# Four single waits in a hybrid decoder step: other score banks, turns ahead of the last scores, forget sums turned at once, idle products at the start

## The chip, the cores and the metric

The kernel runs on one core of one Trainium2 chip. TensorE (PE in the profile, with its weight loads as PEld) multiplies matrices, VectorE (DVE), ScalarE (ACT) and GpSimd (POOL) do the element-wise work, and SyncE (SP) issues most transfers. PSUM, into which PE writes, has eight banks of 128 partitions x 512 float32. The metric is the device time of one execution in microseconds (us), as the median of several runs.

## The reference

One inference step of a two-layer decoder, for a prompt of 2048 positions and for 8 sequences of 4 new positions that have a paged past of 2048. Layer 0 runs two groups of four heads beside each other, a gated linear recurrence ("A") and a forgetting attention ("B", called fox in the code), both from one input projection. Layer 1 is a gated linear attention. Of what the change touches, the reference is this, shortened:

```python
def rmsnorm(x, g):
    y = xf * lax.rsqrt(jnp.mean(xf * xf, axis=-1, keepdims=True) + EPS)
    return y * g

def fox_prompt(q, k, v, log_f):                 # per head, blocks of 128 queries
    c = jnp.cumsum(log_f, axis=1)
    logits = q @ k.T * scale + c[:, None] - c[None, :]
    p = softmax(where(causal, logits, -inf))
    return p @ v

def fox_sample(...):                            # the new positions, on the pages
    suffix_past = lax.cumsum(lf_past, axis=1, reverse=True) - lf_past
    logit_past = q @ k_past.T * scale + cum_new[..., None] + suffix_past[:, :, None, :]
```

Every output is compared with this, in float32. The kernel multiplies float32 values as two float16 parts, a high and a low one, and so three products stand for one (lines L623, L624 and L625 of the kernel before; the helper is `mm3`).

## The kernel before, in words

The program has three stages: `phase_even` (norm of the input, the projections of layer 0 and the recurrence of A), `phase_fox` (the attention B), and the output projection with layer 1. Instructions are written down in one order by Python generators that are merged by estimated costs (the numbers that they yield), and a scheduler then sets each engine's order. Every engine works through its own row in order, and instructions wait for each other by semaphores. A tile with a tag takes the next of the buffers that the tag has; the pool gives a tag its PSUM banks at the first tile with that tag, from the first bank on that is free in the pool's region. A tile that reuses a bank waits for the last reader of the tile before it.

The start. Rows of x are loaded (`nx`), ACT squares them (`nsq`, L451), DVE multiplies them by the reciprocal root (L453), PE turns them in pieces of 128x128 (`nt`, L477), and ACT and DVE split them into the two float16 parts of `act` (L618, L619) with the gain `g_even`. The gain is first scaled by a power of two, for which PE spreads a row over the partitions (`spr_e`, L271) and DVE reduces it (L272). Meanwhile the first weight `w_Ai` is measured (`rm_Ai`, L300) and split (L353 on ACT, L354 on DVE). The first projection is `pt_Av`.

PSUM. In `phase_even` the pool has the tags "pj" (3 banks, the projections), "gr" (2), "st" (1) and "o" (2); the first tile is `spr_e` with "pj". The last projection is the value unit of B: four tiles `pt_Bv` turn over the three "pj" banks, and ACT (L1070) and DVE (L1064, L1071) read them out into `Bv` and `Bvs`. In `phase_fox` a pool that begins at the same first bank has "s" (2 banks, the scores) and "sc" (1, page scores), and another has "t" (2), "o" (1) and "kt" (2). The first tile of the former is a score tile with "s".

Attention. Sixteen groups (head h, group G of four blocks of 128 queries) are worked through. For a block, `scores` multiplies q and k (`s`), DVE adds the bias and takes the maximum (L1413), ACT takes exponentials (L1421, `L3150` is the piece 0 of block 15 of head 3), DVE sums and POOL normalizes (L1429). For a finished group, `values` turns the weights (`pt`, L1449), splits them (`th` on ACT, L1456; `tl` on DVE, L1457) and multiplies them with v into one bank `fo`, from which `fy` (DVE, L1472) reads it out. `values` turns two tiles ahead of the products. The values of a group run beside the scores of the next one; those of the last group run after its scores, in two halves of two blocks (`th3300` is the turn 0 of the first half of head 3 group 3; `th32011` is the turn 11 of head 3 group 2, the last one of that group). At this place ACT and DVE also prepare the output weights `w_o` (L353, L354, L360) and the activations `act` of the output projection (L1814, L1815).

Beside all that, `fox_sample` loads pages of the past with SP, turns the keys (`pkt`, L1573), copies them (`kts`, ACT and DVE) and scores them (`sc`). Between the pages it makes the sums of the log forget values: for each of the four heads it turns one 128x128 tile (`lfT`, L1620), copies it on ACT (`lfTs`, L1622) and multiplies it with two masks into `psf` (L1623, L1624).

## Time and profile before

| what | before |
|---|---|
| runs, median of 3 | 2329.38 us (2325.68 to 2329.55) |
| profiled execution, its own time | 2327.94 us |
| span of the profile | 2326.2 us |
| PE busy | 2248.9 us, 97% of the span |
| DVE, ACT, POOL busy | 1412.1, 1018.5, 733.7 us |
| mean granted clock | 0.991 |

A row of the profile names the start in us, the duration, the engine, the line of the kernel, the operation, the output and input tiles without their numbers, and their shapes. In square brackets stands the idle time of the engine before the row, and what ended it. A row with x4 is four instructions taken together. A stretch of the view by windows gives for each engine the busy time in it, then the mean TensorE clock that was granted (1.00 is full), the busy share of the transfer engines and their rate.

### The profile page before, as it was taken

The numbers are of one execution on the slowest core, as the hardware profiler recorded it, in microseconds if no ns is written. First come the engines' busy times: TensorE is split into PE (matmuls) and PEld (weight loads), VectorE is DVE, ScalarE is ACT, GpSimd is POOL, SyncE is SP. The second block draws the span as 40 slices with busy tenths as digits, with TensorE's granted clock in tenths as the row PEclk, the third lists the DMA queues.
The fourth block names the chain that finished last, engine by engine and source line by source line (L and its number), as shares of the span: only waits on it lengthen the run. The fifth ranks groups of instructions, "written<-read, shape, count | busy, mean of one in ns | idle before, by whom it ended". The sixth has DMA issues, their size and how long they took to land.

```text
span 2326.2 us, 57896 instructions
## 1 busy us (share of the span) xinstructions
PE 2248.9 (97%) x23060; PEld 1604.3 (69%) x23060; DVE 1412.1 (61%) x3281; ACT 1018.5 (44%) x2264; POOL 733.7 (32%) x786
## 2 busy tenths in 40 slices
PE   7999999999999999999999999999999999999998
PEld 5667677855755875565446888677677666666887
DVE  7766568526654657667777445366675655557554
ACT  6434354211222225555566543545544544545343
POOL 2333334001201214223345345144552432322232
PEclk9999999999999999999999999999999999999999
DMA  7343444755432377875983969524234431115553
GB/s 238 120 128 105 146 127 164 201 142 160 143 120 73 125 189 251 245 242 196 276 262 102 335 195 263 132 79 137 74 102 96 121 96 58 49 56 164 176 181 150
DMA packets 357423, 361.64 MB, mean 155 GB/s; under 512 B 105777, under 2 KB 300658, under 8 KB 353058
## 3 DMA queue, kind: packets, MB, share of 16 engines
q1 hardware_dynamic: 355010, 351.33, 49.4%
q0 software_dynamic: 2144, 6.62, 0.8%
q8 instruction: 181, 2.97, 0.5%
q14 instruction: 88, 0.72, 0.1%
HBM read 244.54 MB, written 96.42 MB: 147 GB/s over the span
## 4 chain that ended last, share of the span: by engine, by line
PE 40%; DVE 5%; DMA 2%; ACT 2%; issue 1%; POOL 1%; SPq 1%; POOLq 0%; DVEq 0%; ACTq 0%
PE pt_o L623 4%; PE pt_o L624 4%; PE pt_o L625 4%; PE pt_Cv L623 2%; PE pt_Cv L624 2%; PE pt_Cv L625 2%; PE o_C L910 1%; PE gl_C L756 1%; PE pt L1449 1%; PE pv L1711 1%; DMA yr<-yT 1%; DMA wr_Cv<-in_w_in_odd 1%; PE py_C L728 1%; DVE scT L771 1%; PE fo L623 0%
## 5 line engine op out<-in xcount | busy, mean ns | idle before, releaser
L623 PE MATMUL pt_o<-w_o,act 128*128 128x256 f16 x1024 | 278.9, 273 | 1.9 <-ACT sg1C L680 1.9
L624 PE MATMUL pt_o<-w_o,act 128*128 128x256 f16 x1024 | 278.9, 273 | 0.0
L625 PE MATMUL pt_o<-w_o,act 128*128 128x256 f16 x1024 | 278.7, 273 | 0.0
L623 PEld LDWEIGHTS <-act 128*128 128x128 f16 x2304 | 226.1, 98 | 35.9 <-issue 3.6
L624 PEld LDWEIGHTS <-act 128*128 128x128 f16 x2304 | 226.2, 98 | 32.0 <-issue 3.4
L625 PEld LDWEIGHTS <-act 128*128 128x128 f16 x2304 | 226.2, 98 | 29.9 <-issue 1.7
L790 POOL TENSOR_TENSOR kA<-kA,fA 128x512 f32<-128x512 f32 (+1 forms) x56 | 80.9, 1445 | 344.8 <-PE gl_A L756 273.1
L623 PE MATMUL pt_Cv<-w_Cv,act 128*128 128x256 f16 (+1 forms) x512 | 141.3, 276 | 0.0
L624 PE MATMUL pt_Cv<-w_Cv,act 128*128 128x256 f16 (+1 forms) x512 | 141.3, 276 | 0.0
L625 PE MATMUL pt_Cv<-w_Cv,act 128*128 128x256 f16 (+1 forms) x512 | 141.2, 276 | 0.0
L790 POOL TENSOR_TENSOR kC<-kC,fC 128x512 f32<-128x512 f32 (+1 forms) x56 | 83.6, 1492 | 154.3 <-PE gl_C L756 103.1
L1429 POOL TENSOR_SCALAR L<-L,nm 128x512 f32<-128x512 f32 (+3 forms) x160 | 99.3, 635 | 103.5 <-DVE nm L1425 46.7
L1421 ACT ACTIVATE L<-L,nm,kc 128x512 f32<-128x512 f32 (+3 forms) x160 | 118.2, 740 | 27.5 <-DVE nm L1419 26.3
L1456 ACT ACTIVATE th<-pt 128x512 f16<-128x512 f32 (+3 forms) x159 | 81.8, 528 | 88.3 <-PE pt L1449 86.8
L1457 DVE TENSOR_TENSOR tl<-pt,th 128x512 f16<-128x512 f32 (+3 forms) x159 | 95.0, 609 | 20.7 <-ACT th L1456 18.9
L1449 PE MATMUL pt<-ident,L 128*128 128x128 f32 x544 | 91.4, 280 | 1.4 <-POOL L L1429 0.9
L1573 PEld LDWEIGHTS pkt<-ident,pgcache_fox_k 128*128 128x128 f32 x512 | 59.2, 142 | 44.2 <-issue 27.1
L1573 PE MATMUL pkt<-ident,pgcache_fox_k 128*128 128x128 f32 x512 | 78.5, 281 | 5.7 <-DVE kts L1578 1.7
L1449 PEld LDWEIGHTS pt<-ident,L 128*128 128x128 f32 x544 | 67.7, 144 | 23.3 <-DVE tl L1457 4.5
L1911 ACT ACTIVATE vC<-pt_Cv,kc 128x512 f32<-128x512 f32 (+1 forms) x40 | 23.9, 598 | 129.9 <-PE pt_Cv L625 129.9
L623 PE MATMUL pt_Bk<-w_Bk,act 128*128 128x256 f16 x256 | 70.2, 274 | 1.8 <-DVE Bvs L1071 1.8
L623 PE MATMUL pt_Av<-w_Ai,act 128*128 128x256 f16 x256 | 70.8, 277 | 0.5 <-ACT act L618 0.5
(959 smaller groups left out, 6566.6 us busy)
## 6 DMA issues: line engine op xcount, KB each, us to landing
pgcache_fox_k<-in_cache_fox_k SPq DMA_DIRECT2D x128, 256.0 KB, 4.2
pgcache_fox_v<-in_cache_fox_v SPq DMA_DIRECT2D x128, 256.0 KB, 4.2
yr<-yT SPq DMA_DIRECT2D x16, 1024.0 KB, 7.4
x1d<-xo SPq DMA_DIRECT2D x44, 256.0 KB, 4.7
wr_o<-in_w_out_even SPq DMA_DIRECT2D x32, 256.0 KB, 5.3
xo<-in_x_prompt SPq DMA_DIRECT2D x32, 256.0 KB, 5.5
wr_Cv<-in_w_in_odd SPq DMA_DIRECT2D x32, 256.0 KB, 3.9
x1r<-x1d SPq DMA_DIRECT2D x16, 512.0 KB, 4.9
```

What stands on the lines that cost most here:

```text
L623: nc.tensor.matmul(ps, lh[0], rh[0], start=first, stop=False)
L624: nc.tensor.matmul(ps, lh[0], rh[1], start=False, stop=False)
L625: return nc.tensor.matmul(ps, lh[1], rh[0], start=False, stop=last)
L728: nc.tensor.transpose(py[:, c * rows : (c + 1) * rows], on[:rows, c, t * P : (t + 1) * P], self.ident[:rows, :rows])
L790: nc.gpsimd.tensor_tensor(kv[:, :, 0], kv[:, :, 0], t1.to_broadcast([P, nb, w]), ALU.mult)
L1421: self.last_exp = nc.scalar.activation(lt[:, :w], lt[:, :w], AF.Exp, bias=nm[:, 0:1], scale=ib, accum_out=nm[:, 2 + j : 3 + j])
L1429: nc.gpsimd.tensor_scalar(lt[:, :w], lt[:, :w], nm[:, 1:2], 2.0**14, ALU.mult, ALU.mult)
L1449: nc.tensor.transpose(pt[:, w : w + P], rows[b][s // 4][0][:, (s % 4) * P : (s % 4 + 1) * P], self.ident)
L1456: nc.scalar.activation(th[:, a:w], pt[:, a:w], AF.Copy),
L1457: nc.vector.tensor_tensor(tl[:, a:w], pt[:, a:w], th[:, a:w], ALU.subtract)))
L1573: last = nc.tensor.transpose(pk[:, j * P : (j + 1) * P], pgs[j][:, h * P : (h + 1) * P], self.ident)
L1911: r = nc.scalar.activation(v[h][:, g : g + cnt], ps[:, :, :256], AF.Copy, scale=c)
```

## The change

Four edits, in five places. As the kernel begins, a tile of zeros is set by DVE, and PE multiplies it by itself fifteen times into a PSUM tile with the tag "st" that nobody reads; and the second of the first row tiles is multiplied on ACT and not on DVE. Ahead of the attention, a tile `sc_first` with the tag "sc" is taken and not used, so that "sc" gets its bank before "s" does. In the last group, `values` of the first half is called after the third block's scores as far as its first two turns (`early`), and the rest of it follows after the last block's scores and the values of the group before; the bank `fo` is passed in a list, since it is taken later than the turns. And the four turns of the log forget values go into one tile, which DVE copies in one instruction, then the generator yields 3000, and then the eight products follow.

```diff
@@ norm_groups: prep
-                    nc.vector.tensor_scalar(xt[:n], xt[:n], r, None, ALU.mult)
+                    if c0 == P:
+                        nc.scalar.activation(xt[:n], xt[:n], AF.Copy, scale=r)
+                    else:
+                        nc.vector.tensor_scalar(xt[:n], xt[:n], r, None, ALU.mult)
@@ phase_even
+            warm = wp.tile([P, 512], F32, tag="kt", name="warm").bitcast(F16)
+            nc.vector.memset(warm[:, :512], 0.0)
+            ps = pps.tile([P, 512], F32, tag="st", name="warm")
+            for _ in range(15):
+                nc.tensor.matmul(ps, warm[:, :P], warm[:, :512], start=True, stop=True)
             self.sx_even = self.gain_scale(self.g_even, pps, "pj", "e")
@@ fox_prompt: values
-        def values(h, G, rows, po, b1, b2):
+        def values(h, G, rows, out, b1, b2, early=False):
...
             ahead = [turn(j) for j in range(min(2, nj))]
+            if early:
+                yield 0
+            po = out[0]
             for j in range(nj):
@@ fox_prompt: the groups
         groups = [(h, G) for h in range(NH) for G in range(4)]
+        pps.tile([P, 512], F32, tag="sc", name="sc_first")
         loads(0, 0)
...
+                if j + 1 == len(groups) and b == 2:
+                    po = []
+                    lead = values(h, G, rows, po, 0, 2, True)
+                    next(lead)
             yield from pv
-            po = pps.tile([P, 512], F32, tag="o", name=f"fo{h}{G}")
             if j + 1 < len(groups):
+                po = []
                 pv, ns = values(h, G, rows, po, 0, 4), 4 * (G + 1)
-
-        yield from values(h, G, rows, po, 0, 2)
+            po.append(pps.tile([P, 512], F32, tag="o", name=f"fo{h}{G}"))
+
+        yield from lead
         yield from values(h, G, rows, po, 2, 4)
@@ fox_sample: past
+            pt = pps.tile([P, 512], F32, tag="kt", name="lfT")
+            for h in range(NH):
+                nc.tensor.transpose(pt[:, h * P : (h + 1) * P], lfp[:, :, h], self.ident)
+            lt = fs.tile([P, 512], F32, tag="kt", name="lfTs")
+            nc.vector.tensor_copy(lt, pt)
+            yield 3000
             psf = pps.tile([P, NH, P], F32, tag="kt", name="psf")
             for h in range(NH):
-                pt = pps.tile([P, 512], F32, tag="kt", name=f"lfT{h}")
-                nc.tensor.transpose(pt[:, :P], lfp[:, :, h], self.ident)
-                lt = fs.tile([P, 512], F32, tag="kt", name=f"lfTs{h}")
-                nc.scalar.activation(lt[:, :P], pt[:, :P], AF.Copy)
-                nc.tensor.matmul(psf[:, h], lt[:, :P], stri, start=True, stop=False)
+                nc.tensor.matmul(psf[:, h], lt[:, h * P : (h + 1) * P], stri, start=True, stop=False)
```

The scheduler moves other instructions of the attention stage in consequence. The orders below are those that the two programs have; a row gives its place on the engine, the line, the operation and the tiles with the program's numbers. Lines of the changed kernel are a little further down (L1429 is the exponential that was L1421, L1464 the split that was L1456, L626 the product that was L623).

ACT at the end of head 3 group 2 and the start of the last group, before (`L315` are the exponentials of the last block, `th32` turns of group 2, `th33` turns of the last group):

```order
809 L1456 ACTIVATE th32010_18542<-pt32010_18539 128x256
810 L1456 ACTIVATE th32011_18647<-pt32011_18645 128x128
811 L1421 ACTIVATE L3150_18556,nm315_18633<-L3150_18556,nm315_18633,kc_67 128x512
812 L1421 ACTIVATE L3151_18598,nm315_18633<-L3151_18598,nm315_18633,kc_67 128x512
813 L1421 ACTIVATE L3152_18624,nm315_18633<-L3152_18624,nm315_18633,kc_67 128x512
814 L1421 ACTIVATE L3153_18630,nm315_18633<-L3153_18630,nm315_18633,kc_67 128x512
815 L1456 ACTIVATE th3300_18669<-pt3300_18664 128x512
816 L1456 ACTIVATE th3301_18678<-pt3301_18673 128x512
817 L353 ACTIVATE w_o000_18607<-wr_o000_18600,kc_67 128x512
```

And in the changed kernel:

```order
806 L1464 ACTIVATE th32010_18552<-pt32010_18549 128x256
807 L1464 ACTIVATE th3300_18564<-pt3300_18559 128x512
808 L1429 ACTIVATE L3150_18584,nm315_18641<-L3150_18584,nm315_18641,kc_67 128x512
809 L1429 ACTIVATE L3151_18590,nm315_18641<-L3151_18590,nm315_18641,kc_67 128x512
810 L1429 ACTIVATE L3152_18596,nm315_18641<-L3152_18596,nm315_18641,kc_67 128x512
811 L1429 ACTIVATE L3153_18602,nm315_18641<-L3153_18602,nm315_18641,kc_67 128x512
812 L353 ACTIVATE w_o000_18669<-wr_o000_18662,kc_67 128x512
813 L1464 ACTIVATE th3301_18573<-pt3301_18568 128x512
814 L353 ACTIVATE w_o000_18669<-wr_o000_18662,kc_67 128x512
815 L1464 ACTIVATE th32011_18655<-pt32011_18653 128x128
816 L360 ACTIVATE w_o000_18669<-wr_o000_18662 128x512
```

th3300 has moved ahead of the four exponentials, th32011 behind them and behind two pieces of w_o and th3301. On PE, the product that reads th32011 stands ahead of all products of the last group in both kernels.

DVE at the same place in the changed kernel:

```order
1892 L1433 RECIPROCAL nm315_18641<-nm315_18641 128x1
1893 L354 SCALAR_TENSOR_TENSOR w_o000_18669<-wr_o000_18662,kc_67,w_o000_18669 128x512
1894 L1465 TENSOR_TENSOR tl3301_18574<-pt3301_18568,th3301_18573 128x512
1895 L354 SCALAR_TENSOR_TENSOR w_o000_18669<-wr_o000_18662,kc_67,w_o000_18669 128x512
1896 L1465 TENSOR_TENSOR tl32011_18656<-pt32011_18653,th32011_18655 128x128
1897 L1834 SCALAR_TENSOR_TENSOR act_18640<-yr0000_18667,kc_67,act_18640 128x2x256 x2
1898 L1483 SCALAR_TENSOR_TENSOR fy320_18688<-fo32_18165,kc_67,fsg32_17571 128x512
```

Before, fy320 stood ahead of nm315's sum and reciprocal and of the two w_o and the two act instructions; now it stands behind them.

PE at the log forget sums, before (`lfT` a turn, `psf` the sums, `spr_gh` the next piece of `past`):

```order
10446 L1623 MATMUL psf_11432<-stri_11388,lfTs0_11435 128x128
10447 L1624 MATMUL psf_11432<-tots_11430,mpg_11391 128x128
10448 L1620 MATMUL lfT1_11445<-ident_58,lfp_11386 128x128
10449 L1623 MATMUL psf_11432<-stri_11388,lfTs1_11447 128x128
10450 L1624 MATMUL psf_11432<-tots_11430,mpg_11391 128x128
10451 L1620 MATMUL lfT2_11458<-ident_58,lfp_11386 128x128
10452 L1449 MATMUL pt0200_11909<-ident_58,L0110_11608 128x128
10453 L1449 MATMUL pt0201_11918<-ident_58,L0110_11608 128x128
10454 L1623 MATMUL psf_11432<-stri_11388,lfTs2_11460 128x128
```

And in the changed kernel, where the four turns stand at row 10443 and the rows between are turns and scores:

```order
10466 L1651 MATMUL sc0_11195<-kts030_11362,qz_10936 32x512
10467 L1651 MATMUL sc0_11195<-kts031_11380,qz_10936 32x512
10468 L1651 MATMUL sc0_11195<-kts032_11387,qz_10936 32x512
10469 L1651 MATMUL sc0_11195<-kts033_11394,qz_10936 32x512
10470 L1642 MATMUL psf_11491<-stri_11407,lfTs_11456 128x128
10471 L1643 MATMUL psf_11491<-tots_11449,mpg_11410 128x128
10472 L1642 MATMUL psf_11491<-stri_11407,lfTs_11456 128x128
10473 L1643 MATMUL psf_11491<-tots_11449,mpg_11410 128x128
```

The turn that stood directly ahead of its product on PE is now 26 rows ahead, and the copies that stood on ACT are one copy on DVE.

## The prediction

> **What bounds the kernel now.** I read the busy table first, then TensorE's (PE's) waits, then the same engines in stretches, then the rows of the four places that the change touches.
>
> ```profile
> span 2326.2 us, 57896 instructions
> PE 2248.9 (97%) x23060; PEld 1604.3 (69%) x23060; DVE 1412.1 (61%) x3281; ACT 1018.5 (44%) x2264; POOL 733.7 (32%) x786
> ```
>
> PE is busy for 2248.9 of 2326.2 us, so all that can be won without less matrix work is 77 us of gaps and the time at a lower clock. The other engines count only where PE waits for them. The change removes no matrix work; it adds fifteen idle products and moves the rest. So each part is worth the PE gap that it closes, the gap that it opens, and the half clock behind a gap.
>
> ```profile
> core 0: us, PE busy (x) PEld busy (x) DVE busy (x) ACT busy (x) POOL busy (x), PEclk, DMA share, GB/s
> 0.00:14.90 14.90, 5.47 (x21) 3.83 (x22) 8.48 (x27) 7.09 (x13) 4.32 (x21) 1.00 0.87 306
> ...
> 850.00:857.00 7.00, 3.59 (x33) 2.98 (x32) 3.22 (x7) 1.42 (x3) 0.90 (x2) 0.91 1.00 313
> 857.00:870.00 13.00, 12.23 (x55) 6.09 (x56) 10.18 (x50) 7.33 (x21) 6.50 (x14) 0.79 1.03 232
> ...
> 905.00:915.00 10.00, 7.48 (x41) 5.65 (x41) 4.09 (x11) 5.71 (x15) 4.36 (x8) 0.83 1.02 292
> ...
> 1244.00:1270.00 26.00, 22.39 (x148) 17.14 (x149) 21.33 (x61) 18.49 (x40) 20.42 (x23) 0.87 0.04 14
> ```
>
> The column behind POOL is the granted clock. A mean of 0.83 over 10 us is 3.4 us at half speed (2 x 0.17 x 10); 0.87 over 26 us is 6.8 us; 0.91 over 7 and 0.79 over 13 us together 6.7 us. Work done at half clock takes twice as long, so a stretch full of work loses half its length: 1.7, 3.4 and 3.4 us at most. After each of the three later gaps the clock was halved, and that costs about as much as the gap.
>
> **First scores (other banks): no change, 0 us.**
>
> ```profile
> 856.44 0.48 DVE L1071 SCALAR_TENSOR_TENSOR Bvs<-pt_Bv,kc,Bvs 128x256 f16<-128x256 f32 x1 [0.47 <-ACT Bvs L1070]
> 857.02 0.27 PE L623 MATMUL s<-k,q 128*128 128x128 f16 x1 [3.43 <-DMA vn<-vs]
> ```
>
> PE stands still for 3.43 us. The row blames a small load, but the matmul starts 0.1 us after the DVE row that reads pt_Bv for the last time (856.44 + 0.48 = 856.92): the scores' first bank is the one that the last value group still holds. The new `sc_first` takes one bank ahead of the scores and moves them from the first and second bank of the region to the second and third. That would clear the clash if the value groups stayed in place. But `warm` is now the first PSUM tile of the phase before and claims the region's first bank for the tag "st", so the three "pj" banks that pt_Bv turns over also move one up. The last pt_Bv moves from the first bank to the second, and so do the scores. The two edits cancel, the same instruction waits for the same evacuation, and its 3.43 us and the half clock behind it remain. Bounds: 0, and, should the banks not clash, a gain of 3.4 plus up to 3.4.
>
> **Log forget sums: -3.5 us.**
>
> ```profile
> 908.21 0.25 ACT L1622 ACTIVATE lfTs<-lfT 128x128 f32<-128x128 f32 x1
> ...
> 905.47 0.49 PE L1623 MATMUL psf<-stri,lfTs 128*128 128x128 f32 x2 [0.37 <-ACT lfTs L1622]
> 908.52 0.49 PE L1623 MATMUL psf<-stri,lfTs 128*128 128x128 f32 x2 [2.00 <-ACT lfTs L1622]
> 909.72 0.49 PE L1623 MATMUL psf<-stri,lfTs 128*128 128x128 f32 x2 [0.15 <-ACT lfTs L1622]
> ```
>
> The third copy of a turned head stands on ACT behind the four exponentials of one score block, and PE needs it at once. In the new order the four turns are issued together, DVE copies them in one instruction, and 26 PE rows (turns, scores, page products) lie between those turns and the first sum. I count 0.37 + 2.00 + 0.15 = 2.5 us of gap and 1.7 us of clock, 4.2 in all, as the most. DVE gets one copy of 128x512 in its queue ahead of a score's bias-and-maximum; by the nearest DVE row below (fy, same shape, 0.75 us) this can hold PE up for 0.75 us. I take -3.5; the bounds are -4.2 and 0 (if another small wait keeps the clock down).
>
> **Last group: +4 us.**
>
> ```profile
> 1258.81 0.37 PE L623 MATMUL fo<-th,v 128*128 128x256 f16 x1 [2.97 <-ACT th L1456]
> 1259.54 0.37 PE L624 MATMUL fo<-tl,v 128*128 128x256 f16 x1 [0.35 <-DVE tl L1457]
> ...
> 1257.39 0.80 ACT L1421 ACTIVATE L<-L,nm,kc 128x512 f32<-128x512 f32 x1
> 1258.19 1.05 ACT L1456 ACTIVATE th<-pt 128x512 f16<-128x512 f32 x2
> 1259.14 0.71 ACT L353 ACTIVATE w_o<-wr_o,kc 128x512 f16<-128x512 f32 x1
> 1259.76 1.06 ACT L1456 ACTIVATE th<-pt 128x512 f16<-128x512 f32 x2
> 1261.84 1.33 ACT L1814 ACTIVATE act<-yr,kc 128x512 f16<-128x512 f32 x2
> ...
> 1255.44 0.75 DVE L1472 SCALAR_TENSOR_TENSOR fy<-fo,kc,fsg 128x512 f32<-128x512 f32 x1 [0.49 <-PE fo L625]
> 1262.89 2.27 DVE L1815 SCALAR_TENSOR_TENSOR act<-yr,kc,act 128x512 f16<-128x512 f32 x2
> ```
>
> Now, the last turn of head 3 group 2 (th32011) is copied ahead of the last block's four exponentials, fo32 ends, fy empties its bank, and then PE waits 2.97 + 0.35 us for th3300, which stands behind the exponentials. The change brings th3300 ahead of them, as it says. But the turn that is pushed back is th32011: on ACT it now comes after the four exponentials, two pieces of w_o and th3301. PE runs in order, so fo32's last product holds up all that follows.
>
> I count from the end of th3300. On ACT: four exponentials at 0.80 (3.2), two w_o at 0.62 (from 1259.14 to 1259.76), th3301 at half of 1.05, th32011 about 0.2 (a quarter of the width): 5.2 us. PE has five products and seven turns before that wait, by my estimate 1.4 us (0.10 to 0.16 each at full clock), of which 0.5 pass before th3300 ends: cover 0.9. So a gap of 4.3 us or, if the exponentials also start late by 0.5, 4.8; I take 4.5. Then a second wait: fo33 needs the one "o" bank that fy320 empties, and fy320 now stands on DVE behind the two act instructions (2.27 us), which wait for ACT's act (one w_o piece and half of 1.33 after th32011). So 5.2 + 0.5 + 0.7 = 6.4, + 2.27 + 0.75 = 9.4 us, while PE has some 16 short products, 1.7 us at full clock and 3.4 at half: idle 0.8 to 2.5, I take 1.5. Gaps of 6.0 replace 3.3: +2.7. The clock stays half over a hole of 8.5 us with little in it, and then until a full stretch of work: 0 to 1.7 more than now, I take +0.7. The block before may also hold th3208 back by 0 to 1.4, I take +0.6. Sum +4. Bounds: -1.7 (gaps as now, one 3.4-us stretch at half clock less) and 4.0 + 1.7 + 1.4 = +7.1.
>
> **Beginning: +0.5 us.**
>
> ```profile
> 8.17 1.11 PE L477 MATMUL nt<-ident,nx 128*128 128x128 f32 x4 [3.72 <-DVE nx L453]
> 14.87 0.42 PE L623 MATMUL pt_Av<-w_Ai,act 128*128 128x256 f16 x1
> 16.11 0.42 PE L623 MATMUL pt_Av<-w_Ai,act 128*128 128x256 f16 x1
> 16.32 0.42 PE L624 MATMUL pt_Av<-w_Ai,act 128*128 128x256 f16 x1
> ...
> 19.59 0.27 PE L625 MATMUL pt_Av<-w_Ai,act 128*128 128x256 f16 x1
> 19.69 0.27 PE L623 MATMUL pt_Av<-w_Ai,act 128*128 128x256 f16 x1
> ...
> 10.53 0.68 DVE L300 TENSOR_REDUCE rm_Ai<-wr_Ai 128x1 f32<-128x512 f32 x1
> 11.19 1.57 ACT L618 ACTIVATE act<-nt,g_even 128x256 f16<-128x256 f32 x4 [3.41 <-PE nt L477]
> 23.06 1.20 ACT L618 ACTIVATE act<-nt,g_even 128x256 f16<-128x256 f32 x3 [3.96 <-PE nt L477]
> ```
>
> At 16.11 one product follows another after 0.21 us, at 19.59 after 0.10 (the clock column does not show this stretch, the rows do). From 14.87 to some 19.3 us pt_Av so runs at half clock, and some 2.2 us are lost there. The warm products could save them, but by my estimate they end by about 7 us (fifteen of 512 columns at 0.42 each, twice the 0.21 of the 256-column rows), and PE then has only the turns until 14.9: it is busy for 5.47 of the first 14.90 us. The trace shows how little idle time is enough: with the 2.00-us gap before 908.52 came the half clock that the 905 to 915 stretch shows. So I expect half clock again when pt_Av starts. Against the products: spr_e stands behind them on PE and its reduction behind the weight reductions on DVE, the last of which ends at 11.2. The gain g_even, which ACT needs at 11.19, then comes after that and a handful of short steps, by my estimate 1 us later than it is needed now. For it, ACT takes over one normalization multiply from DVE, and the w_Ai splits come ahead of four turns. What sets the pace after 20 us is the next rows' squares and splits on ACT and DVE (ACT waits 3.96 us before 23.06), not PE. Bounds -2.2 and +2.0; I take +0.5.
>
> The Trainium skill ("TensorE: Matmul & The Clock Gate", Part 1) says that the clock falls only after a whole idle window of about 3.4 us. By that rule the warm clock would last through the turns and the 2.2 us would be saved at the start. The rows here disagree: 2.00 us with work on both sides sufficed.
>
> **Sum.** 0 - 3.5 + 4 + 0.5 = +1.0 us against the profiled execution, 2327.94 us (span 2326.2), so 2328.9. That execution is 1.4 us below the median of the runs, 2329.38, which is what the result is held against: 2330.4, I say 2330. The scheduler also reorders the rest of the attention stage (the same products, other neighbours; page loads are waited for there): unknown, 3 us either way. From the output projection on the two orders are the same. A change below 0.2% (4.7 us) can't be told from none.
>
> **Rivals.**
> 1. *The last group's hole is not longer than now and the sums give all they can.* PE's waits are exchanged one for one, a stretch of half clock falls away: -4.2 - 1.7 + 0 = -5.9, 2323.5. For it: th3300 does come ahead. Against: the ACT order above.
> 2. *All four waits go, as the change says*: -3.4 - 3.4 - 4.2 - 3.3 - 3.4 - 2.2 = -20, 2309. Against: the banks and the order; I know of no way for it.
> 3. *Slower: fo32's last product decides.* Place: the end of head 3 group 2. Price: the upper bound +7.1, with the start at +1.5 and the sums at -2.5: +6.1, 2335.5. It decides from the point where the gap before fo33 lets the clock fall twice.
> 4. *The start's clock holds* (the page's rule as a mechanism): -2.2 at most instead of +0.5 gives 2327.7, the same verdict.
>
> **How the numbers follow.** Forecast 0.47 (own range 2325 to 2334), start's clock holding 0.06, rival 1 0.18, rival 2 0.02, rival 3 0.27. Faster comes from rivals 1 and 2 and the forecast's lower edge, 0.21; slower from rival 3 and the upper edge, 0.28; the same 0.51. The range runs from just below rival 1 to beyond rival 3, 2321 to 2339.
>
> **What would show it.** Right: the first score's wait of about 3.4 us still there behind Bvs with half clock after it; no gap above 0.5 us at psf and clock 1.00 around it; ahead of fo32's last product a PE wait of 4 to 5 us for th, and a second, for fy, ahead of fo33; pt_Av's first products still at a pitch of 0.21 us. Wrong: a first score without a wait (I have misread the banks), a th32011 that does not wait for the exponentials, or gaps among the page turns that outweigh all four places.

## The result, and the profile after

The changed kernel takes 2346.38 us (median of 7 runs, 2342.76 to 2348.53) against 2329.38 us (7 runs, 2325.52 to 2338.47): a ratio of 1.0072 [1.0059, 1.0085]. It is slower by 17 us. The forecast was 2330 us, no change that can be measured, with a range up to 2339; the time lies outside it, and beyond rival 3 (2335.5) too. Of the runs reported below, one of twelve of the kernel g3 (2379.79 us) and one of twelve of the kernel h2 (4056.62 us) were in a slow state, and the ratios leave these two out.

The profiled execution of the changed kernel took 2346.38 us itself, with a span of 2344.3. From the first part of its page:

```profile
span 2344.3 us, 57930 instructions
PE 2259.6 (96%) x23075; PEld 1608.7 (69%) x23075; DVE 1408.7 (60%) x3282; ACT 1017.7 (43%) x2261; POOL 732.1 (31%) x786
```

The span is 18.1 us longer, and PE is busy for 10.7 us more, though only fifteen short products were added (6.2 us, as shown below). So part of the loss is work at a lower clock and part is gaps.

To place it, the same products were looked up in the two traces, by their tiles and the order in which they come, at five points; how much later each is than in the first profile of before gives what a stage lost. "Start" ends at 75 us; "middle" ends with the last value group (pt_Bv, 853 us before); "pages" reaches from there to the last page turn (oT, 1244.5 us before); "tail" from there to the product that stood at 1300 us, in the output projection; "behind" is the rest. A few product records are missing from every trace, so a value holds to some 0.4 us.

| us later than before | start | middle | pages | tail | behind | sum |
|---|---|---|---|---|---|---|
| changed kernel | 2.7 | 3.6 | -5.5 | 13.4 | 4.0 | 18.1 |
| kernel before, a second profile | 0.4 | 4.2 | -4.3 | -0.1 | 6.7 | 7.0 |

The second row is the kernel before itself, profiled once more. It has the same 4 us in the middle and 6.7 us behind. So of the changed kernel's 18.1 us, the middle and the end need not be the change's; what is surely its own is the start and, above all, the tail. The tail in the view by windows, before:

```profile
1244.50:1300.00 55.50, 52.04 (x435) 42.78 (x434) 41.75 (x88) 42.29 (x84) 40.32 (x41) 0.94 0.58 184
```

And in the changed kernel, between the same two products:

```profile
1245.20:1314.10 68.90, 57.60 (x448) 44.60 (x447) 39.15 (x93) 43.87 (x87) 38.35 (x40) 0.93 0.50 157
```

PE stood idle for 3.5 us of that stretch before, and for 11.3 us now. Not all of the 13.4 us is loss: the stretch holds 13 more products (x448 against x435). They are score products, turns and value products that stood ahead of the last page turn before. By my estimate they take some 2.4 us at full clock: six of 512 columns at 0.21 us (half of the 0.41 us that one takes at half clock at the start), three of 384 columns at 0.16 us and four turns (0.66 us). The pages look better by as much. The longest groups of PE's waits in the whole execution (total us, times, longest one), in the changed kernel:

```profile
PE pv L1730 <- DMA pgcache_fox_v<-in_cache_fox_v: 9.1, 5, 3.0
PE fo L626 <- DVE fy L1483: 5.1, 2, 4.9
PE fo L626 <- ACT th L1464: 5.0, 3, 4.0
...
PE s L626 <- DMA vn<-vs: 3.0, 1, 3.0
```

and before, for the same groups:

```profile
PE fo L623 <- ACT th L1456: 3.8, 2, 3.0
PE s L623 <- DMA vn<-vs: 3.4, 1, 3.4
PE pv L1711 <- DMA pgcache_fox_v<-in_cache_fox_v: 2.6, 3, 1.1
PE psf L1623 <- ACT lfTs L1622: 2.5, 3, 2.0
```

The waits at psf are gone. The waits at the last group (fo) and for value pages (pv) have grown, and the wait of the first score is still there. The last group in the changed kernel, in order of time, PE, ACT, DVE and SP's queue:

```profile
1263.20 0.27 PE L626 MATMUL fo<-th,v 128*128 128x128 f16 x1 [3.99 <-ACT th L1464]
1266.88 0.27 PE L626 MATMUL fo<-th,v 128*128 128x256 f16 x1 [0.18 <-DVE fy L1483]
1281.66 0.39 PE L626 MATMUL fo<-th,v 128*128 128x256 f16 x1 [4.92 <-DVE fy L1483]
...
1260.40 0.80 ACT L1429 ACTIVATE L<-L,nm,kc 128x512 f32<-128x512 f32 x1
1262.89 0.26 ACT L1464 ACTIVATE th<-pt 128x128 f16<-128x128 f32 x1
1279.70 1.33 ACT L1833 ACTIVATE act<-yr,kc 128x512 f16<-128x512 f32 x2 [4.62 <-DMA yr<-yT]
...
1280.45 0.75 DVE L1834 SCALAR_TENSOR_TENSOR act<-yr,kc,act 128x512 f16<-128x512 f32 x1 [4.32 <-ACT act L1833]
1281.12 0.48 DVE L1483 SCALAR_TENSOR_TENSOR fy<-fo,kc,fsg 128x256 f32<-128x256 f32 x1
...
1272.07 17.54 SPq L1820 DMA_DIRECT2D yr<-yT  x4
1289.67 2.38 SPq L335 DMA_DIRECT2D wr_o<-in_w_out_even  x4
```

Three things are to be seen. PE's first hole, 3.99 us, ends 0.05 us after th32011's copy, which stands on ACT behind the exponentials: the hole that was forecast. Its second, 4.92 us, was not: the product waits for fy330, which on DVE stands behind an act instruction, and this one waits for a reload of yT, the attention's result, that the output projection takes back in. And on SP's queue four reloads take 17.54 us, and the next weight wr_o is issued only at 1289.67. Before, the same queue read:

```profile
1270.40 2.59 SPq L1801 DMA_DIRECT2D yr<-yT  x2
1273.40 2.30 SPq L335 DMA_DIRECT2D wr_o<-in_w_out_even  x4
```

The weight was 16 us earlier there. SP's order shows why. Before, the rows are three reloads, the weight, and further work; the reloads for the second half (yr_19795 and yr_19797) come 20 rows later:

```order
1065 L1801 DMA yr_18968<-yT_81 128x8x32
1066 L335 DMA wr_o_18939<-in_w_out_even 128x2x256 x4
...
1087 L1801 DMA yr_19795<-yT_81 128x8x256
1088 L1801 DMA yr_19797<-yT_81 128x8x256
```

In the changed kernel those two stand ahead of the weight:

```order
1064 L1820 DMA yr_18978<-yT_81 128x8x32
1065 L1820 DMA yr_19805<-yT_81 128x8x256
1066 L1820 DMA yr_19807<-yT_81 128x8x256
1067 L335 DMA wr_o_18949<-in_w_out_even 128x2x256 x4
```

The first of them takes the buffer of an earlier reload and so waits until POOL has made its act from that one; everything behind it on SP waits too.

### The profile page after: what moved, and what is told of

The parts are those of the page before. It is cut to its first block, busy times and chain, and to the rows that moved or that the text cites. A ratio compares the mean times of both kernels' runs of the same rounds, so it can differ in the third digit from the quotient of the medians.

```text
span 2344.3 us, 57930 instructions
## 1 busy us (share of the span) xinstructions
PE 2259.6 (96%) x23075; PEld 1608.7 (69%) x23075; DVE 1408.7 (60%) x3282; ACT 1017.7 (43%) x2261; POOL 732.1 (31%) x786
## 4 chain that ended last, share of the span: by engine, by line
PE 41%; DVE 4%; DMA 3%; POOL 1%; ACT 1%; issue 1%; SPq 1%; POOLq 0%; DVEq 0%; ACTq 0%
PE pt_o L626 4%; PE pt_o L627 4%; PE pt_o L628 4%; PE pt_Cv L626 2%; PE pt_Cv L627 2%; PE pt_Cv L628 2%; PE pv L1730 1%; DMA yr<-yT 1%; PE o_C L913 1%; PE gl_C L759 1%; PE pt L1457 1%; DMA pgcache_fox_v<-in_cache_fox_v 1%; PE fo L626 1%; PE fo L628 1%; PE fo L627 1%
## 5 line engine op out<-in xcount | busy, mean ns | idle before, releaser
L626 PE MATMUL pt_o<-w_o,act 128*128 128x256 f16 x1024 | 279.8, 274 | 1.3 <-ACT sg1C L683 1.3
L626 PEld LDWEIGHTS <-act 128*128 128x128 f16 x2304 | 226.7, 98 | 37.3 <-issue 3.6
L626 PE MATMUL pt_Cv<-w_Cv,act 128*128 128x256 f16 (+1 forms) x512 | 141.4, 276 | 0.0
L1429 ACT ACTIVATE L<-L,nm,kc 128x512 f32<-128x512 f32 (+3 forms) x160 | 118.2, 741 | 27.7 <-DVE nm L1427 24.3
L1464 ACT ACTIVATE th<-pt 128x512 f16<-128x512 f32 (+3 forms) x159 | 81.8, 528 | 100.9 <-PE pt L1457 95.9
L626 PE MATMUL pt_Bk<-w_Bk,act 128*128 128x256 f16 x256 | 71.3, 279 | 1.9 <-DVE Bvs L1074 1.9
L626 PE MATMUL pt_Av<-w_Ai,act 128*128 128x256 f16 x256 | 70.8, 276 | 0.9 <-ACT act L621 0.9
```

The lines of the kernel that those rows point to most:

```text
L626: nc.tensor.matmul(ps, lh[0], rh[0], start=first, stop=False)
L1429: self.last_exp = nc.scalar.activation(lt[:, :w], lt[:, :w], AF.Exp, bias=nm[:, 0:1], scale=ib, accum_out=nm[:, 2 + j : 3 + j])
L1464: nc.scalar.activation(th[:, a:w], pt[:, a:w], AF.Copy),
```

## The experiments

Each time is a median, and each ratio is to the kernel before, run beside it on the same chip. The stages are those of the table above, always against the first profile of before.

| kernel | time us (runs) | ratio [95%] | start | middle | pages | tail | behind |
|---|---|---|---|---|---|---|---|
| start alone (e1) | 2335.5 (12) | 1.0022 [1.0008, 1.0037] | 1.9 | 5.1 | -1.2 | -0.2 | 2.9 |
| banks alone (e2) | 2332.78 (12) | 1.0009 [0.9997, 1.0022] | 0.7 | 1.0 | -0.2 | 1.4 | 8.6 |
| sums alone (e3) | 2339.32 (6) | 1.0039 [1.0024, 1.0054] | 0.4 | 4.4 | -3.0 | 12.7 | -0.9 |
| last group alone (e4) | 2342.11 (6) | 1.0057 [1.0036, 1.0078] | 0.1 | 2.3 | 1.5 | 9.5 | -0.4 |
| sums, no yield (f5) | 2326.07 (12) | 0.9984 [0.9972, 0.9996] | 0.3 | 2.5 | -8.1 | 0.3 | 2.9 |
| last group, one piece beside (f6) | 2339.7 (6) | 1.0037 [1.0024, 1.0050] | 0.9 | 1.7 | 0.2 | 12.7 | 4.0 |
| whole, no yield (f7) | 2344.77 (8) | 1.0048 [1.0031, 1.0066] | 3.7 | 2.4 | -2.7 | 10.5 | 2.7 |
| nx on ACT alone (f8) | 2334.88 (1) | one run | 0.1 | 2.7 | 0.4 | -0.2 | 3.7 |
| before again (g1) | 2334.91 (1) | one run | 0.4 | 4.2 | -4.3 | -0.1 | 6.7 |
| last group, drained (g2) | 2334.47 (12) | 1.0009 [0.9994, 1.0023] | 0.7 | 2.7 | 0.1 | -0.2 | 5.8 |
| f5 and g2 (g3) | 2325.89 (12) | 0.9979 [0.9962, 0.9996] | 0.0 | 1.6 | -6.9 | 0.1 | 3.9 |
| f5 and e2 (g4) | 2328.6 (12) | 0.9996 [0.9981, 1.0011] | -0.1 | 3.8 | -4.0 | 0.8 | 2.2 |
| whole, drained (h1) | 2345.37 (6) | 1.0068 [1.0052, 1.0083] | 1.2 | 5.7 | -2.5 | 13.2 | 0.8 |
| whole, drained, no yield (h2) | 2332.23 (12) | 1.0013 [0.9999, 1.0026] | 2.5 | 1.6 | -4.1 | -0.7 | -3.0 |
| e3, reloads held (i1) | 2331.71 (12) | 1.0003 [0.9989, 1.0017] | -0.3 | 2.2 | -3.3 | 5.4 | -2.3 |
| e4, reloads held (i2) | 2336.87 (12) | 1.0028 [1.0011, 1.0044] | 0.4 | 0.2 | -0.7 | 8.7 | -2.5 |
| whole, reloads held (i3) | 2340.68 (12) | 1.0032 [1.0018, 1.0046] | 2.1 | 4.9 | -5.2 | 12.8 | 4.3 |
| whole, drained and held (i4) | 2336.01 (12) | 1.0012 [0.9999, 1.0026] | 2.4 | 5.2 | -3.9 | 4.2 | 5.0 |

### One edit at a time (e1 to e4)

Each kernel is the one before with one of the four edits, as the diff of the change has it. Start alone:

> The kernel before with the idle products and the multiply moved to ACT, alone. Theory: the profile after shows the first products about 2.7 us late and no gain behind it, so +2.7 at the start; but the tile of the idle products moves the value groups' banks by one while the scores stay in the first bank, so the first score's wait of 3.4 us falls to under 0.5, with up to 3.4 us of clock. Sum -0.7 to -4.1: 2325 to 2329. Rival (the banks have nothing to do with that wait): wait still 3 us, 2332.

Banks alone:

> The kernel before with sc_first alone, so that the scores' first bank is not the one of the last value group. Theory: the first score's wait of 3.4 us falls to under 0.5 and the half clock behind it goes in part: -3.4 to -6.8, 2323 to 2326. Rival (it waits for the load that the row names): 2329, wait as before.

Sums alone:

> The kernel before with the forget sums turned at once, alone. Theory: the 2.5 us of gaps and 1.7 us of half clock there go, nothing comes in their place: -3.5 to -4.2, 2325 to 2326. Rival: the larger cost that this generator now yields makes it run ahead or behind the prompt's, so that value pages come late as in the changed kernel (gaps of 3.0 and 2.5 us near 1203 and 1212, and half clock): +1 to +4, 2330 to 2333.

Last group alone:

> The kernel before with the last group's turns ahead, alone. Theory: holes of some 4 us for th32011 and 5 us for fy330 (behind an act instruction that waits for a reload of yT), with half clock for 10 us in place of 7: +7 to +10, 2336 to 2339. Rival (what the changed kernel lost there is small, most of its 17 us is clock and late pages elsewhere): +2 to +4, 2331 to 2333.

Three of the four are slower alone: the last group by 0.57%, the sums by 0.39%, the start by 0.22%; the banks make no measurable difference. Sums and last group have the same long tail, 12.7 and 9.5 us, and the whole change has it once (13.4), not twice. That speaks for one shared cause there. None of the four took the time that was expected of it: all four lie above their ranges, and in e1 and e2 the first scores' gain did not come.

The sums alone are the surprise, since their own place gained. With the sums alone the first wait of the last group is about that of before (3.09 us for th), a later product waits 1.61 us for th besides, and the largest new wait in the tail is for the weight. PE, then SP, in e3:

```profile
1297.06 0.37 PE L623 MATMUL pt_o<-w_o,act 128*128 128x256 f16 x1 [4.78 <-ACT w_o L360]
...
1272.05 13.12 SPq L1803 DMA_DIRECT2D yr<-yT  x4
1285.22 4.44 SPq L335 DMA_DIRECT2D wr_o<-in_w_out_even  x4
```

SP has the early reloads here too, and the first output product waits 4.78 us for the weight that came late.

The banks. In e2 the scores have left the bank of the last value group, and yet nothing is won. PE and DVE in e2:

```profile
855.05 0.22 PE L623 MATMUL s<-k,q 128*128 128x128 f16 x1
858.40 0.48 PE L623 MATMUL s<-k,q 128*128 128x384 f16 x1 [2.69 <-DVE mx L1413]
...
857.66 0.49 DVE L1071 SCALAR_TENSOR_TENSOR Bvs<-pt_Bv,kc,Bvs 128x256 f16<-128x256 f32 x1 [0.47 <-ACT Bvs L1070]
858.06 0.28 DVE L1413 CUSTOM_DVE_ANT_0 L<-s,cm 128x128 f32<-128x128 f32 x1
```

The first two scores start at once, but there are two score banks, and the third score needs the first one read out. DVE does that at 858.06, behind the evacuation of the last value group at 857.66. The wait has only moved, from 3.43 to 2.69 us. In e1, where the products at the start move the last pt_Bv one bank up and the scores stay, the second score meets it in the same way. PE in e1:

```profile
860.35 0.22 PE L626 MATMUL s<-k,q 128*128 128x128 f16 x1
863.50 0.28 PE L626 MATMUL s<-k,q 128*128 128x256 f16 x1 [2.82 <-DVE Bvs L1074]
```

### The yield, the piece beside, and the start (f5 to f8)

```diff
# f5, from e3; f7, from the whole change
-            yield 3000
# f6, from e4: which pieces of act are made beside the last group
-                for steps in pieces[:2]:
+                for steps in pieces[:1]:
...
-                for steps in pieces[2:]:
+                for steps in [pieces[1][1:]] + pieces[2:]:
# f8, from before: the second row tile is multiplied on ACT, nothing else
```

> The kernel before with the forget sums turned at once, but without the new cost of 3000 that the generator yields. Theory: that cost, not the turns, makes the merged order of the whole stage another one (506 rows of DVE stand elsewhere with it, 58 without), and the late value pages and the wait before the output projection come from there. Without it the three waits at psf (2.5 us) and the half clock there go and nothing else changes: 3 to 4 us less than before, 2325 to 2327, value-page gaps near 1200 under 1 us each. Rival (the one copy on DVE, or the turns ahead, delay the pages): 2336 to 2341, like the sums with the cost.

> The kernel before with the last group's turns ahead, and the second piece of the output activations taken out of the stretch beside it (it follows behind the last turns). Theory: the act instruction that waits for the reload of yT no longer stands ahead of fy330 on DVE, so the hole of 4 us there goes with 3.4 us of half clock; the hole at th32011 of 3.3 us stays: 2333 to 2337, against 2342 with the last-group edit alone. Rival (fy330 waits for something else): gap of 4 us stays, 2340 to 2344.

> The whole change without the cost of 3000. Theory: the page gaps of 3.0 and 2.5 us near 1203 and 1212 go with their half clock, the two holes of the last group (4.0 and 4.9 us) stay: 2338 to 2341. Rival (the late pages come from another part of the change): 2345 to 2348, gaps still there.

> The kernel before with one normalization multiply on ACT and no idle products: one look at the start. Theory: the products delay spr_e and with it g_even; without them PE is at 75 us within 0.7 us of before. Rival (the multiply on ACT is what delays): 1.5 to 2.7 us late at 75 us.

f5 is faster than before, 0.9984 [0.9972, 0.9996], some 4 us. Without the yield the turns and the one copy stay, the waits at psf are gone as well, and the tail is 0.3 us. So the edit of the sums itself does what it says, and the 3000 that it yields costs more than it wins: the number goes into the merge of the generators, and with it the order of the whole attention stage changes, down to SP's reloads. It is the yield, too, that makes the value pages late: PE's waits for them are 8.3 to 9.9 us in the six kernels that have it (the changed one, e3, h1, i1, i3 and i4) and 1.4 to 3.4 us in all others.

f6 takes the act away that stood ahead of fy330. The tail stays at 12.7 us. PE in f6:

```profile
1298.31 0.37 PE L623 MATMUL pt_o<-w_o,act 128*128 128x256 f16 x1 [6.15 <-ACT w_o L360]
```

The hole ahead of fy330, 4.05 us in e4, is gone, and PE waits for the weight instead. So that hole was cover for the late weight, and removing it alone wins nothing that can be told: the intervals of e4 and f6 overlap. f6 and f7 were expected at 2333 to 2337 and 2338 to 2341 us and are above that.

f7 shows that the yield isn't the only way to the early reloads: with the undrained last group SP has them there too, tail 10.5 us. f8 has no loss at the start (0.1 us) where e1 has 1.9 us, so what costs there comes with the products and not with the multiply.

### The last group drained, and what is best (g1 to g4)

In g2 the values of the group before are finished before the last turns are taken, so that th32011 is again ahead of the exponentials:

```diff
# g2, from e4
                 if j + 1 == len(groups) and b == 2:
+                    yield from pv
                     po = []
# g3: f5 and g2. g4: f5 and e2. g1: the kernel before, unaltered
```

> The kernel before itself, unaltered, for one more look. Theory: outside the stages that the change touches, the changed kernel lost 3.5 us from 75 to 853 us and 4.0 us behind the attention in half-clock stretches alone, and those fall by chance, since the same instructions meet the clock's windows at another phase. So this run too differs from the first profile there, by 2 us or more, with half-clock stretches in other places. Rival (those 7.5 us are a cost of the change): at the same instructions within 0.5 us of the first profile, same half-clock stretches.

> The kernel before with the last group's turns ahead, but the values of the group before drained first, so that th32011 stands ahead of the last exponentials again (th3300 comes one exponential earlier than before the change). Theory: th32011 behind the exponentials was what opened the holes; now there is one hole, of 2.0 to 2.5 us for th3300, and no other: 2328 to 2331, the same as before. Rival (any turn ahead of the last scores costs, since work is taken from beside them): holes of 3 to 5 us as with the edit as it was, 2338 to 2343.

> The forget sums turned at once without the cost of 3000, and the drained last group. Theory: both gains add, 2324 to 2326. Rival (the drained group costs in this order): 2329 to 2334.

> The forget sums turned at once without the cost of 3000, and sc_first; every engine's order is that of the sums alone. Theory: the first scores start at once, but the third waits for DVE, which still reads out the last value group, so the first stretch gains 0.3 to 1 us only: 2324 to 2327, no different from the sums alone (2326). Rival (the freed wait counts in full): 2320 to 2323.

g2's tail is that of before, -0.2 us, with one long hole left. PE in g2:

```profile
1261.48 0.27 PE L623 MATMUL fo<-th,v 128*128 128x256 f16 x1 [2.18 <-ACT th L1456]
```

2.18 us instead of 2.97: the drained form closes less than one microsecond of the wait it was meant for, and as a whole it can't be told from before, 1.0009 [0.9994, 1.0023]. SP has the order of before in g2. g3 is the best kernel of all, 0.9979 [0.9962, 0.9996], but its interval and that of f5 overlap almost fully, so the drained last group is not shown to add anything. g4 isn't better than f5: the freed bank gives no gain.

g1 is what tells how much one profile is worth; it is read at the end.

### The drained change, and the reloads held back (h1, h2, i1 to i4)

In the i kernels the reloads for the second half are issued only behind the last weight load of the first half, which puts the weight on SP ahead of them again, as before the change; on ACT, DVE and POOL few rows move.

```diff
# i1 from e3, i2 from e4, i3 from the whole change, i4 from h1
-                    nc.sync.dma_start(t["raw"]...)
+                    self.last_fetch = nc.sync.dma_start(t["raw"]...)
...
-            pieces = load(self.y_pieces(1, 0, act, wpool))
+            with tc.issue_after(self.last_fetch.ins):
+                pieces = load(self.y_pieces(1, 0, act, wpool))
# h1: the whole change with g2's line. h2: h1 without the yield
```

> The whole change, with the values of the group before drained ahead of the last group's turns, so that th32011 stands ahead of the last exponentials; the cost of 3000 stays. Theory A (the last group's order is the main cost of the change): the holes of 4.0 and 4.9 us go, from the last page turn to the output projection 56 to 58 us as before the change instead of 69: 2333 to 2337. Theory B (the cost of 3000 alone makes as long a tail, as in the forget sums alone, 68 us): holes of 3 to 5 us stay ahead of the output projection: 2342 to 2347.

> The whole change, drained as in the run before and without the cost of 3000: idle products, multiply on ACT, sc_first and sums stay. Theory: what is left is the start (2 to 3 us late), the first scores (nothing won) and the sums (4 us won): 2326 to 2331, tail 55 to 57 us. Rival (a third cause is still in it): 2334 or more.

> The forget sums turned at once with the cost of 3000, and two reloads of yT for the second half (yr0100, yr010256) held on SP behind the loads of the output weights. Theory C: in every kernel with a long tail SP has these two reloads ahead of the load of the second output weight (wr_o001), and they wait for a buffer, so that the weight's load is issued 12 to 15 us late; held back, the wait of 4.8 us ahead of the output projection goes and the tail is 55.5 to 58 us in place of 68: 2327 to 2331, against 2339 without the hold. Rival (late work on ACT and DVE makes the tail): tail 65 us or more, 2337 to 2341.

> The last group's turns ahead, alone, with the same two reloads held. Theory C: the queue takes part of the tail of 65 us, th32011 and fy330 the rest: holes of 3.3 and 4.0 us stay, the output projection no longer waits behind them, tail 59 to 62 us, 2333 to 2337, against 2342. Rival (the holes alone make the tail): 65 us, 2341 to 2343. Second rival (the holes come from the queue too): tail 55.5 to 57, 2328 to 2331.

> The whole change with the same two reloads held. Theory C: tail 60 to 63 us in place of 69, since the holes of 4.0 and 4.9 us stay: 2338 to 2341. Rival (the holes alone make it): 69 us, 2345 to 2347.

> The whole change, drained, with the same two reloads held and the cost of 3000 still in it. Theory C: both causes of the tail are gone, tail 55.5 to 58 us, the late value pages of 2 to 2.6 us stay: 2330 to 2335, against 2345 with the drain alone. Rival (the cost of 3000 has another way to the tail): 2341 to 2346.

In h1 the last group's extra holes are gone, and its tail is still 13.2 us, since the reloads are early. PE and SP in h1:

```profile
1300.30 0.27 PE L626 MATMUL pt_o<-w_o,act 128*128 128x256 f16 x1 [5.03 <-ACT w_o L360]
...
1275.88 13.06 SPq L1821 DMA_DIRECT2D yr<-yT  x4
1289.00 3.28 SPq L335 DMA_DIRECT2D wr_o<-in_w_out_even  x4
```

SP in i1, the sums with the reloads held:

```profile
1268.84 2.59 SPq L1803 DMA_DIRECT2D yr<-yT  x2
1271.55 2.56 SPq L335 DMA_DIRECT2D wr_o<-in_w_out_even  x4
```

The weight is early again, the tail falls from e3's 12.7 to 5.4 us and the ratio from 1.0039 [1.0024, 1.0054] to 1.0003 [0.9989, 1.0017]. With the drained change (h1 to i4) the tail falls from 13.2 to 4.2 us and the ratio from 1.0068 [1.0052, 1.0083] to 1.0012 [0.9999, 1.0026]. In both pairs the tail's fall, 7.3 and 9.0 us, is about the fall of the medians, 7.6 and 9.4; the ratios, each to runs of before on the same chip, fall by 8.4 and 13.0 us. So SP's order is shown to be the cause of that much. All four tails are still 2 to 5 us longer than was expected of the held kernels.

For the whole change the two causes cover one another. Drained alone (h1) the tail is 13.2 us, held alone (i3) 12.8, both (i4) 4.2: either one suffices for the long tail. In i3's trace PE no longer waits for the weight; the two holes of the last group, 3.99 us for th and 5.28 us for fy, are there. One thing doesn't fit: i3's ratio, 1.0032 [1.0018, 1.0046], is clearly better than the whole change's, though its profiled tail is no shorter. i3's profiled execution, 2347.11 us, lies at the upper end of its runs, so it can't say where the typical run gains; i2 against e4 is the same puzzle, and with overlapping intervals (1.0028 [1.0011, 1.0044] and 1.0057 [1.0036, 1.0078]). Dropping the yield as well (h2) leaves the ratio where i4 has it, 1.0013 [0.9999, 1.0026], with a tail of -0.7 us. Of what remains of i1's and i4's tails, some 2.4 us is the moved work named above; the rest has not been followed up. Why the scheduler moves the reloads is not settled either: it was only seen that it does so with the yield or with the undrained last group, in all six kernels with a long tail whose reloads were not held, and in none of the others.

## Why the prediction was wrong, by its steps

**First scores: 0 us, right; its upper bound wrong.** The two edits cancel as worked out. PE and DVE in the changed kernel:

```profile
862.84 0.22 PE L626 MATMUL s<-k,q 128*128 128x128 f16 x1 [3.03 <-DMA vn<-vs]
...
862.25 0.49 DVE L1074 SCALAR_TENSOR_TENSOR Bvs<-pt_Bv,kc,Bvs 128x256 f16<-128x256 f32 x1 [0.47 <-ACT Bvs L1073]
```

The score starts 0.1 us after Bvs, as before. But "should the banks not clash, a gain of 3.4 plus up to 3.4" was no bound: e2 has no clash and waits 2.69 us for DVE. With two score banks the third score needs DVE, and DVE is late with or without the clash.

**Log forget sums: -3.5 us, right for the place, and the step that left out the yield failed.** In the changed kernel's windows the stretch around psf is full, at full clock:

```profile
903.00:915.00 12.00, 12.00 (x90) 8.58 (x89) 9.98 (x37) 7.25 (x19) 3.87 (x7) 1.00 0.85 294
```

f5, the edit without the yield, has the forecast's size: 0.16% of 2330 is 3.7 us. But the yield of 3000 was read as part of this place. The yield's effect on the order went into "the rest of the attention stage [...] unknown, 3 us either way", and it was larger: e3 minus f5 is 13 us in the medians. One piece of it is seen among the pages of the changed kernel, where value pages are loaded later against their use:

```profile
1206.26 1.05 PE L1730 MATMUL pv<-pgcache_fox_v,pT 128*16 128x512 f32 x8 [3.02 <-DMA pgcache_fox_v<-in_cache_fox_v]
1214.34 1.05 PE L1730 MATMUL pv<-pgcache_fox_v,pT 128*16 128x512 f32 x8 [2.52 <-DMA pgcache_fox_v<-in_cache_fox_v]
```

Those are 5.5 us of gaps where before the longest was 1.1. The larger piece is SP's order. With that held (i1) the sums are at 1.0003, still 0.19% (4 us) above f5, and the late pages are still in it; the intervals of these two overlap.

**Last group: +4 us; the first hole right, the rest not.** The hole ahead of th32011's product was forecast at 4.5 us and is 3.99. The second wait, for fy320, was forecast at 1.5 us and is 0.18. The third hole, 4.92 us, was not foreseen: the DVE order was read as far as fy320, and not as far as fy330, which stands behind the next act in the changed kernel and ahead of it before. It is the same mechanism that was used for fy320, an evacuation behind an act that waits for something else, one group further on. It waited for a transfer, and so it was longer. The drained form (g2) removes it together with the first hole's growth. The upper bound of +7.1 was too small: e4 alone is at +0.57%, 13 us. What it lacked is mainly the queue: with the reloads held (i2) the last group is at +0.28%, 6.5 us, inside the bound, though the two intervals overlap.

**"From the output projection on the two orders are the same": wrong, and this is the step that failed most.** It holds for PE's products behind the projection's start, but SP's queue into the projection wasn't replayed. Two reloads had moved ahead of a weight, one of them waits for a buffer, and the weight came 16 us late. This cost is shown with e3 and i1, 7 to 8 us, and with h1 and i4, 9 us. It stood in the order of SP before any run.

**Beginning: +0.5 us, a size that was off.** The products are the first rows of PE in the changed kernel:

```profile
1.30 6.18 PE L1140 MATMUL warm<-warm 128*128 128x512 f16 x15 [1.30 <-DVE warm L1137]
8.16 0.66 PE L480 MATMUL nt<-ident,nx 128*128 128x128 f32 x4 [0.46 <-DVE nx L456]
10.63 1.12 PE L480 MATMUL nt<-ident,nx 128*128 128x128 f32 x4 [1.81 <-ACT nx L454]
...
15.18 0.42 PE L626 MATMUL pt_Av<-w_Ai,act 128*128 128x256 f16 x1
```

Fifteen products take 6.18 us, 0.41 each, as estimated. The four turns at 8.16 run at full clock (0.66 us), the four at 10.63 at half (1.12), and pt_Av starts at half clock as foretold, at 15.18 instead of 14.87. The granted clock in the two stretches beside the drop:

```profile
6.95:10.36 3.41, 1.41 (x9) 0.82 (x7) 3.01 (x6) 1.76 (x3) 0.92 (x2) 1.00 1.06 387
10.36:17.19 6.83, 4.86 (x22) 3.93 (x23) 5.70 (x20) 4.67 (x10) 0.00 (x0) 0.50 1.04 405
```

The half clock comes back although PE was busy for 1.41 of the 3.41 us before it. The net price is 2.7 us here, 1.9 alone, and 2.1 to 3.7 in the other kernels that have the products, apart from h1 (1.2): just beyond the upper bound of 2.0, against +0.5. The kernels without them have -0.3 to 0.9 there. e1's ratio, 1.0022 [1.0008, 1.0037], or 1.9 to 8.6 us, includes that price.

Rival 4, the clock held through the turns, did not come about. The Trainium skill ("TensorE: Matmul & The Clock Gate", Part 1) has the clock fall after a whole idle window of some 3.4 us. This trace disagrees: 3.41 us with work in 41% of them sufficed.

Where the price comes from can be read on DVE. PE and DVE before:

```profile
27.78 0.33 PE L477 MATMUL nt<-ident,nx 128*128 128x128 f32 x1 [0.57 <-DVE act L619]
27.73 0.16 DVE L269 TENSOR_REDUCE kc<-g_odd 128x1 f32<-128x8 f32 x1
```

And in the changed kernel:

```profile
29.99 0.33 PE L480 MATMUL nt<-ident,nx 128*128 128x128 f32 x1 [2.27 <-DVE act L622]
27.84 0.16 DVE L269 TENSOR_REDUCE kc<-g_odd 128x1 f32<-128x8 f32 x1 [2.10 <-DMA g_odd<-in_norm_odd]
```

The reduction of layer 1's gain, `g_odd`, has moved on DVE ahead of a multiply of `nx` and of the `act` row that this turn waits for, and it waits for its own load. So PE waits 1.7 us more here. It stands so in all seven kernels with the products, where PE waits 1.45 to 2.99 us at this turn, least in h1, which has the smallest price; in the other thirteen traces it stands behind those rows, and no turn near it waits longer than 1.27 us. No run moves this row alone, so that is read from the traces and not shown by an experiment. The delay that was forecast, the gain g_even 1 us later, is there as well: the first act starts on ACT at 12.73 in place of 11.19 us, but it puts pt_Av back by 0.3 us only.

**The rivals.** Rival 3 had the right sign and place with the wrong object: not the products of fo32 decide but fy330 and the weight. Rivals 1 and 2 failed at th32011 and at the banks. The signs named for a right forecast were nearly all seen (only the second wait, 0.18 us, hardly), and the time was still wrong, since none of them stood on SP or in DVE's order at the start.

**The sum.** Forecast 0 - 3.5 + 4 + 0.5 = +1.0. Measured alone, by their ratios to 2330 us: banks +2.1 (not told from none), sums +9.1, last group +13.3, start +5.1, 29.6 together; the whole is at +16.8, which fits sums and last group paying for the same tail.

## What to carry to other kernels

When a change moves work on one engine, replay every queue up to the next stage, the transfer queue first: a load that waits for a buffer holds up all loads behind it, and here that cost 7 to 9 us. A cost that is yielded to a planner is an edit of the whole schedule, so try the edit without it: the same sums are faster by 0.16% without the 3000 and slower by 0.39% with it. Before a bank is freed or a hole closed, name the next thing that is late: the freed bank led to DVE, and the closed hole to the weight. The same goes for a row that waits for a load on any other engine: at the start one such row on DVE, moved forward, is by the traces the larger part of the price.

## What the runs showed of the hardware that was not expected

The same program has its stretches at half clock in other places from one execution to the next, and that is worth several microseconds per stage. Two stretches in which the order is the same in all three traces, in the first profile of before:

```profile
75.00:853.30 778.30, 768.34 (x8672) 540.76 (x8671) 455.96 (x1073) 226.72 (x559) 173.45 (x139) 1.00 0.45 137
1300.00:2320.00 1020.00, 997.08 (x10919) 762.36 (x10916) 579.66 (x1095) 479.58 (x1009) 365.76 (x305) 1.00 0.43 132
```

in its second profile (g1):

```profile
75.40:858.00 782.60, 772.20 (x8673) 542.38 (x8671) 456.19 (x1073) 226.85 (x559) 173.19 (x139) 0.99 0.45 137
1300.30:2327.00 1026.70, 1003.02 (x10919) 765.12 (x10916) 579.42 (x1095) 479.95 (x1008) 366.10 (x305) 0.99 0.44 131
```

In the changed kernel these stretches take 781.8 and 1023.9 us. The same products take 4.3 and 6.7 us longer in the second profile of the same kernel, and most of it is PE busy time at a clock of 0.99 instead of 1.00. Single runs of before lay between 2321.88 and 2343.99 us over four chips. On one of them, beside the i kernels, the three runs with a mean granted clock of 0.988 took 2336.77 to 2343.99 us, and the three with 0.993 took 2326.18 to 2331.74. The forecast was made against a profile in which these two stretches went well, and the pages badly (4.3 us). It also means that a loss of several microseconds in a long stage, read from one profile, is no finding: "behind" alone lies between -3.0 and 8.6 us in the table. Two stages stand above this. The tail lies between -0.7 and 1.4 us in the nine kernels without its two causes, and the start between -0.3 and 0.9 us in those without the products, against 1.2 to 3.7 in the seven with them. The Trainium skill (the same page and part) says that the clock's window runs free of the kernel and that the same kernel therefore differs from run to run; the two profiles agree with that, though no run here sets the window's phase and so none shows that it is the cause.
